# A batched 90-degree rotation: loads and stores on two queues with two pools of buffers, in place of one queue and units passed on

## The chip, the cores and the metric

The kernel runs on one core of one Trainium2 chip. The metric is the device time in microseconds (us). The kernel before was run six times; the median is 123.95 us.

## The reference

```python
def setup_inputs():
    batch, c, h, w = 32, 3, 256, 256
    return {"x": np.random.randn(batch, c, h, w).astype(np.float32)}

def reference(x):
    return np.rot90(x, k=-1, axes=(-2, -1)).astype(np.float32)
```

Each of the 96 images of 256 x 256 float32 values is turned by 90 degrees. Nothing is computed; 25.17 MB are read and 25.17 MB are written.

## The kernel before

The images are handled in 12 slabs of eight images, 2.10 MB each. A slab lies in SBUF as 128 partitions of 16 KB. It is loaded by two DMAs of 1 MB (`i` = 0 and 1), turned by two VectorE transposes of 128 x 2048 values, and stored to the output.

There are two forms of a slab. Slabs 0 and 11 (`last`) are loaded with 8 rows of an image in each partition (L63): a DMA is 128 pieces of 8 KB, and each of the two halves can be transposed by itself (L73). Slabs 1 to 10 are loaded with 16 rows in each partition (L65): a DMA is 64 pieces of 16 KB, one for every second partition, and a transpose (L79) needs both loads of its slab. Each of the two transposes of such a slab writes half of the columns `c` of both halves `i`, so both must be done before either half can be stored. Stores always go out in pieces of 8 KB, apart from the first.

All DMAs are issued by SyncE (SP), on one queue: first the 24 loads, then the stores in the order of the slabs 1 to 11, then slab 0. There is a buffer ("unit") for each of the 12 slabs, so no load waits for a buffer. Slab `n` is turned from its own unit into the unit of slab `n - 1`, whose data have been turned by then:

```python
t_in, t_out = units[n], units[n - 1] if n else turned0
```

Slab 0 has no unit before it: it is turned into `turned0` in PSUM. When slab 11 has been turned, ScalarE copies `turned0` into the unit of slab 11 (L92), from which slab 0 is stored at the very end (L93). Slab 1 is stored by three DMAs (L82 to L84), the first of which is short: 1 KB of each partition, 128 KB in all. Slabs 2 and 3 are stored by two DMAs each (L87), the others by one of 2 MB (L89).

The framework that builds the program sets the waits. It hands out eight semaphores for the completion of DMAs in turn. A DMA that gets a semaphore again waits, on its issuing engine, until the DMA that had it before has landed. With one queue that is the DMA eight places earlier.

Of the kernel before, what the change touches and what calls it, by code (L numbers as in the profile page):

```python
# [1 line left out]

# [4 lines left out]

@with_exitstack
def kernel(
    ctx: ExitStack,
    tc: tile.TileContext,
    x: bass.AP,
    out: bass.AP,
):

    nc = tc.nc
    fp32 = mybir.dt.float32

    B, C, H, W = x.shape
    P = nc.NUM_PARTITIONS  # L40
    RI, RO = 16, 8
    K = H // RI
    I = 2
    Q = P // (K * I)
    n_slabs = B * C // (Q * I)
    last = n_slabs - 1
    F = RO * W

    rows_in = x.rearrange("b c h w -> (b c h) w")
    rows_out = out.rearrange("b c h w -> (b c h) w")  # L50
    ld8_v = rows_in.rearrange("(n i p r) w -> n p i (r w)", i=I, p=P, r=RO)
    ld16_v = rows_in.rearrange("(n i m r) w -> n i m (r w)", i=I, m=Q * K, r=RI)
    st_v = rows_out.rearrange("(n i p c) w -> n p i (c w)", i=I, p=P, c=RO)

    pools = [ctx.enter_context(tc.tile_pool(name=f"unit{u}", bufs=1)) for u in range(n_slabs)]
    units = [pool.tile([P, I, F], fp32, name=f"u{u}") for u, pool in enumerate(pools)]
    psum = ctx.enter_context(tc.tile_pool(name="psum", bufs=1, space=bass.MemoryType.PSUM))
    turned0 = psum.tile([P, I, F], fp32, name="turned0")

    for n in range(n_slabs):  # L60
        for i in range(I):
            if n in (0, last):
                nc.sync.dma_start(out=units[n][:, i], in_=ld8_v[n][:, i])  # L63
            else:
                nc.sync.dma_start(out=units[n][i::I].rearrange("p i f -> p (i f)"), in_=ld16_v[n, i])  # L65

    for n in range(n_slabs):
        t_in, t_out = units[n], units[n - 1] if n else turned0
        if n in (0, last):
            for i in range(I):  # L70
                src = t_in[:, i].rearrange("p (r g c) -> p c r g", r=RO, c=RO)
                dst = t_out[:, i].rearrange("p (c g r) -> p c r g", c=RO, r=RO)
                nc.vector.transpose(out=dst[:, :, ::-1, ::-1], in_=src)  # L73
        else:
            src = t_in.rearrange("p i f -> p (i f)").rearrange("p (r g c) -> p c r g", r=RI, c=RO)
            dst = t_out.rearrange("p i (c k r) -> p c r k i", c=RO, r=RI)[:, :, ::-1, ::-1, :]
            for h in range(2):
                cs = slice(h * RO // 2, (h + 1) * RO // 2)
                nc.vector.transpose(out=dst[:, cs], in_=src[:, cs])  # L79

        if n == 1:
            nc.sync.dma_start(out=st_v[n][:, 0, :W], in_=t_out[:, 0, :W])  # L82
            nc.sync.dma_start(out=st_v[n][:, 0, W:], in_=t_out[:, 0, W:])
            nc.sync.dma_start(out=st_v[n][:, 1], in_=t_out[:, 1])  # L84
        elif n in (2, 3):
            for i in range(I):
                nc.sync.dma_start(out=st_v[n][:, i], in_=t_out[:, i])  # L87
        elif n:
            nc.sync.dma_start(out=st_v[n], in_=t_out)  # L89

    for i in range(I):
        nc.scalar.copy(out=units[last][:, i], in_=turned0[:, i])  # L92
    nc.sync.dma_start(out=st_v[0], in_=units[last])  # L93


# [1 line left out]
_INS = ['x']  # L97
_OUTS = [((32, 3, 256, 256), 'float32')]


# [23 lines left out]
```

## Time and profile before

| what | value |
|---|---|
| six runs | median 123.95 us, 123.61 to 124.03 |
| the profiled execution's own time | 123.88 us |
| its span in the profile | 122.1 us |
| VectorE (DVE) busy | 93.4 us (76%), 24 instructions |
| ScalarE (ACT) busy | 5.0 us (4%), 3 instructions |
| DMA | 50.33 MB, mean 412 GB/s over the span |

The span is the profiled part of that execution; 1.78 us of its own time lie around it. "DMA" in the profile is the mean busy share of the 16 DMA engines of the core, which carry out the transfers of every queue. "Packets" are the pieces that these engines move. An issue on SP ("SPq") only starts a transfer; "landing" is the time at which its completion was signalled.

### The profile page before, as it was taken

The page shows a single profiled execution, that of the slowest core. Times are in us where ns is not written, and L with a number is a line of the kernel's source. Part 1 is how long each engine was busy: PE and PEld are TensorE (multiplying, and loading weights), DVE is VectorE, ACT ScalarE, POOL GpSimd, SP SyncE. Part 2 cuts the span into 40 slices and gives each one's busy share as a digit, 9 for nine tenths or more (in the row PEclk, how much of TensorE's full clock was granted, in tenths as well). Part 3 has the DMA queues.
Part 4 walks back from the last instruction along what each step waited for, and adds up shares of the span by engine and source line. Part 5 has one row for each costly group of instructions (what it writes and reads, how often), then busy time and mean ns, then how long its engine had stood idle before and what let it go on. Part 6 is the DMA issues. An engine that isn't in the chain of part 4 may idle for free.

```text
span 122.1 us, 138 instructions
## 1 busy us (share of the span) xinstructions
DVE 93.4 (76%) x24; ACT 5.0 (4%) x3; POOL 0.2 (0%) x4
## 2 busy tenths in 40 slices
DVE  0199999999999999999999999999999950000000
ACT  0000000000000000000400000000000641000000
POOL 0000000000000000000000000000000000000000
DMA  3999999999999999999999999999999999999994
GB/s 89 429 432 429 429 429 429 429 429 429 429 429 429 429 429 429 429 429 421 384 402 430 427 427 429 429 429 429 427 427 429 429 427 429 427 429 429 429 427 180
DMA packets 5633, 50.33 MB, mean 412 GB/s; under 512 B 641, under 2 KB 769, under 8 KB 897
## 3 DMA queue, kind: packets, MB, share of 16 engines
q1 hardware_dynamic: 5632, 50.33, 97.8%
q14 instruction: 1, 0.00, 0.0%
HBM read 25.17 MB, written 25.17 MB: 412 GB/s over the span
## 4 chain that ended last, share of the span: by engine, by line
DVE 47%; issue 27%; DMA 4%; DVEq 3%; ACT 2%
DVE u L79 37%; DVE turned L73 6%; DMA u<-in_x_dram 4%; DVE u L73 3%; DVEq L119 3%; ACT u L92 2%
## 5 line engine op out<-in xcount | busy, mean ns | idle before, releaser
L79 DVE STREAM_TRANSPOSE u<-u 128x2048 f32<-128x2048 f32 x20 | 78.1, 3954 | 0.3
L73 DVE STREAM_TRANSPOSE turned<-u 128x2048 f32<-128x2048 f32 x2 | 7.6, 3830 | 5.5 <-DMA u<-in_x_dram 5.5
L73 DVE STREAM_TRANSPOSE u<-u 128x2048 f32<-128x2048 f32 x2 | 7.7, 3947 | 0.0
L92 ACT COPY u<-turned 128x2048 f32<-128x2048 f32 x2 | 3.7, 1865 | 36.7 <-DVE u L73 36.7
L92 ACT ACT_TABLE_LOAD x1 | 1.3, 1283 | 59.5 <-DMA u<-in_x_dram 59.5
L108 POOL MEMSET const-bfloat16-1.0<- 128x1 bf16 x1 | 0.1, 101 | 0.0
L108 POOL MEMSET const-uint8-127<- 128x1 uint8 x1 | 0.1, 101 | 0.0
L108 POOL MEMSET const-float32-0.0<- 128x1 f32 x1 | 0.1, 98 | 0.2 <-issue 0.2
L108 POOL MEMSET const-float32-1.0<- 128x1 f32 x1 | 0.1, 98 | 0.0
## 6 DMA issues: line engine op xcount, KB each, us to landing
u<-in_x_dram SPq DMA_DIRECT2D x24, 1024.0 KB, 19.6
out_dram<-u SPq DMA_DIRECT2D x9, 2048.0 KB, 22.9
out_dram<-u SPq DMA_DIRECT2D x5, 1024.0 KB, 17.8
out_dram<-u SPq DMA_DIRECT2D x1, 896.0 KB, 17.8
out_dram<-u SPq DMA_DIRECT2D x1, 128.0 KB, 18.2
```

The lines of the kernel that those rows point to most:

```text
L73: nc.vector.transpose(out=dst[:, :, ::-1, ::-1], in_=src)
L79: nc.vector.transpose(out=dst[:, cs], in_=src[:, cs])
L92: nc.scalar.copy(out=units[last][:, i], in_=turned0[:, i])
L108: nc = _bacc.Bacc("TRN2", target_bir_lowering=False, num_devices=1)
L119: with _tile.TileContext(nc) as tc:
```

## The change

The twelve units and the PSUM tile are replaced by two pools of six buffers each, `t_in` and `t_out`, every buffer 16 KB in each partition. Each slab takes a new buffer from both. SyncE issues the 24 loads, and ScalarE issues 24 stores of 1 MB each, in the order of the slabs from 0 to 11, each slab's two stores after its transposes. Slab 11 is loaded in the 16-row form; only slab 0 keeps the 8-row form. The three-part store of slab 1, the 2 MB stores, and the copies on ScalarE are gone.

```diff
-    pools = [ctx.enter_context(tc.tile_pool(name=f"unit{u}", bufs=1)) for u in range(n_slabs)]
-    units = [pool.tile([P, I, F], fp32, name=f"u{u}") for u, pool in enumerate(pools)]
-    psum = ctx.enter_context(tc.tile_pool(name="psum", bufs=1, space=bass.MemoryType.PSUM))
-    turned0 = psum.tile([P, I, F], fp32, name="turned0")
+    in_pool = ctx.enter_context(tc.tile_pool(name="in_pool", bufs=6))
+    out_pool = ctx.enter_context(tc.tile_pool(name="out_pool", bufs=6))
 
     for n in range(n_slabs):
-        for i in range(I):
-            if n in (0, last):
-                nc.sync.dma_start(out=units[n][:, i], in_=ld8_v[n][:, i])
-            else:
-                nc.sync.dma_start(out=units[n][i::I].rearrange("p i f -> p (i f)"), in_=ld16_v[n, i])
-
-    for n in range(n_slabs):
-        t_in, t_out = units[n], units[n - 1] if n else turned0
-        if n in (0, last):
+        t_in = in_pool.tile([P, I, RO * W], fp32, tag="t_in")
+        t_out = out_pool.tile([P, I, RO * W], fp32, tag="t_out")
+        if n == 0:
             for i in range(I):
+                nc.sync.dma_start(out=t_in[:, i], in_=ld8_v[n, i])
                 src = t_in[:, i].rearrange("p (r g c) -> p c r g", r=RO, c=RO)
                 dst = t_out[:, i].rearrange("p (c g r) -> p c r g", c=RO, r=RO)
                 nc.vector.transpose(out=dst[:, :, ::-1, ::-1], in_=src)
         else:
+            t_flat = t_in.rearrange("p i f -> p (i f)")
+            for i in range(I):
+                nc.sync.dma_start(out=t_flat[i::I], in_=ld16_v[n, i])
...
-        if n == 1:
-            nc.sync.dma_start(out=st_v[n][:, 0, :W], in_=t_out[:, 0, :W])
-            nc.sync.dma_start(out=st_v[n][:, 0, W:], in_=t_out[:, 0, W:])
-            nc.sync.dma_start(out=st_v[n][:, 1], in_=t_out[:, 1])
-        elif n in (2, 3):
-            for i in range(I):
-                nc.sync.dma_start(out=st_v[n][:, i], in_=t_out[:, i])
-        elif n:
-            nc.sync.dma_start(out=st_v[n], in_=t_out)
-
-    for i in range(I):
-        nc.scalar.copy(out=units[last][:, i], in_=turned0[:, i])
-    nc.sync.dma_start(out=st_v[0], in_=units[last])
+        for i in range(I):
+            nc.scalar.dma_start(out=st_v[n, i], in_=t_out[:, i])
```

In the built program the loads settle on four of the eight completion semaphores and the stores on the other four: a load waits for the load four places earlier, a store for the store four places earlier. There is one crossing: the eighth load (the second of slab 3) waits for the second store of slab 0.

More of the change, by code (lines that the diff above doesn't have):

```diff
@@ L45 @@
     n_slabs = B * C // (Q * I)
-    last = n_slabs - 1
-    F = RO * W
     rows_in = x.rearrange("b c h w -> (b c h) w")
     rows_out = out.rearrange("b c h w -> (b c h) w")
-    ld8_v = rows_in.rearrange("(n i p r) w -> n p i (r w)", i=I, p=P, r=RO)
+    ld8_v = rows_in.rearrange("(n i p r) w -> n i p (r w)", i=I, p=P, r=RO)
     ld16_v = rows_in.rearrange("(n i m r) w -> n i m (r w)", i=I, m=Q * K, r=RI)
-    st_v = rows_out.rearrange("(n i p c) w -> n p i (c w)", i=I, p=P, c=RO)
-    pools = [ctx.enter_context(tc.tile_pool(name=f"unit{u}", bufs=1)) for u in range(n_slabs)]
-    units = [pool.tile([P, I, F], fp32, name=f"u{u}") for u, pool in enumerate(pools)]
-    psum = ctx.enter_context(tc.tile_pool(name="psum", bufs=1, space=bass.MemoryType.PSUM))
-    turned0 = psum.tile([P, I, F], fp32, name="turned0")
-    for n in range(n_slabs):
-        for i in range(I):
-            if n in (0, last):
-                nc.sync.dma_start(out=units[n][:, i], in_=ld8_v[n][:, i])
-            else:
-                nc.sync.dma_start(out=units[n][i::I].rearrange("p i f -> p (i f)"), in_=ld16_v[n, i])
-    for n in range(n_slabs):
-        t_in, t_out = units[n], units[n - 1] if n else turned0
-        if n in (0, last):
+    st_v = rows_out.rearrange("(n i p c) w -> n i p (c w)", i=I, p=P, c=RO)
+    in_pool = ctx.enter_context(tc.tile_pool(name="in_pool", bufs=6))
+    out_pool = ctx.enter_context(tc.tile_pool(name="out_pool", bufs=6))
+    for n in range(n_slabs):
+        t_in = in_pool.tile([P, I, RO * W], fp32, tag="t_in")
+        t_out = out_pool.tile([P, I, RO * W], fp32, tag="t_out")
+        if n == 0:
             for i in range(I):
+                nc.sync.dma_start(out=t_in[:, i], in_=ld8_v[n, i])
                 src = t_in[:, i].rearrange("p (r g c) -> p c r g", r=RO, c=RO)
@@ L74 @@
         else:
-            src = t_in.rearrange("p i f -> p (i f)").rearrange("p (r g c) -> p c r g", r=RI, c=RO)
+            t_flat = t_in.rearrange("p i f -> p (i f)")
+            for i in range(I):
+                nc.sync.dma_start(out=t_flat[i::I], in_=ld16_v[n, i])
+            src = t_flat.rearrange("p (r g c) -> p c r g", r=RI, c=RO)
             dst = t_out.rearrange("p i (c k r) -> p c r k i", c=RO, r=RI)[:, :, ::-1, ::-1, :]
```

## The prediction

> **What bounds the kernel now.** I read the page first (slices, DMA queue, groups), then the stretches around the start, the middle and the end of the transfers, then SP's waits.
>
> ```profile
> DMA  3999999999999999999999999999999999999994
> GB/s 89 429 432 429 429 429 429 429 429 429 429 429 429 429 429 429 429 429 421 384 402 430 427 427 429 429 429 429 427 427 429 429 427 429 427 429 429 429 427 180
> DMA packets 5633, 50.33 MB, mean 412 GB/s; under 512 B 641, under 2 KB 769, under 8 KB 897
> ...
> q1 hardware_dynamic: 5632, 50.33, 97.8%
> ```
>
> The 16 DMA engines are full from the second slice to the last but one. One queue carries everything, so loads and stores never lie in the engines side by side, save at the crossing around 60 us.
>
> ```profile
> 20.00:30.00 10.00, 9.93 (x4) 0.00 (x0) 0.00 (x0) 1.00 1.00 426
> 75.00:85.00 10.00, 9.93 (x4) 0.00 (x0) 0.00 (x0) 1.00 1.01 429
> ```
>
> These are the stretches of loads alone and of stores alone (last columns: DMA share, GB/s). Both directions run at the same rate; I use 428 GB/s. 50.33 MB at that rate are 117.6 us.
>
> ```profile
> 58.00:59.00 1.00, 1.00 (x1) 0.00 (x0) 0.00 (x0) 1.00 0.99 410
> 59.00:60.00 1.00, 1.00 (x1) 0.52 (x1) 0.00 (x0) 1.00 0.98 369
> 60.00:61.00 1.00, 0.97 (x2) 0.77 (x1) 0.00 (x0) 1.00 0.99 369
> 61.00:62.00 1.00, 1.00 (x1) 0.00 (x0) 0.00 (x0) 1.00 0.96 365
> ...
> 120.50:120.75 0.25, 0.00 (x0) 0.00 (x0) 0.00 (x0) 1.00 0.24 98
> 120.75:121.00 0.25, 0.00 (x0) 0.00 (x0) 0.00 (x0) 1.00 0.01 0
> ```
>
> At the crossing the rate falls to about 368 GB/s for 3 us. By the page's slices 18 to 20 this costs (8 + 45 + 27) / 429 x 3.05 us = 0.57 us; by the three stretches 0.42 us. I use 0.5 us. The last data move at 120.6 us; the span ends 1.5 us later. So data begin at 120.6 - 117.6 - 0.5 = 2.5 us. Time = end of data + 1.5 + 1.78 (123.88 - 122.1). The profiled execution lies 0.07 us below the median of 123.95.
>
> ```profile
> 0.72 0.86 SPq L63 DMA_DIRECT2D u<-in_x_dram  x2
> ...
> 5.54 7.57 DVE L73 STREAM_TRANSPOSE turned<-u 128x2048 f32<-128x2048 f32 x2 [5.54 <-DMA u<-in_x_dram]
> ...
> L79 DVE STREAM_TRANSPOSE u<-u 128x2048 f32<-128x2048 f32 x20 | 78.1, 3954 | 0.3
> ...
> L92 ACT COPY u<-turned 128x2048 f32<-128x2048 f32 x2 | 3.7, 1865 | 36.7 <-DVE u L73 36.7
> ```
>
> From the first issue to the first data are 2.5 - 0.72 = 1.8 us. The first 1 MB (1.05 MB / 428 = 2.45 us) ends at 4.95, and DVE starts at 5.54: 0.6 us from last byte to the transpose. VectorE needs 7.93 us for a slab (two of 3.954 us and a gap), while the engines need 4.9 us for its loads and 4.9 us for its stores, 9.8 us together. DVE is not the bound, but it is 10.3 us (0.6 + 7.93 + 1.8) from a slab's last loaded byte to its first stored byte.
>
> ```profile
> SPq L65 <- DMA u<-in_x_dram: 25.5, 13, 2.0
> ```
>
> SP waits for the completion semaphore of the DMA eight places back, at up to 2.0 us a time. With eight DMAs of 1 MB in flight these waits cost nothing.
>
> **The change, part by part.**
>
> Gone, at nothing: the two copies of 1.87 us and the table load of 1.28 us on ScalarE. The last store was issued at 101.2 us and landed 20.1 us later, queued behind others all that time. Slab 11's other form changes nothing either (3947 against 3954 ns), nor do slab 0's transposes into SBUF (3830 to about 3947 ns, 0.2 us on an engine with 25 us to spare). If DVE became the bound, these 0.2 us would count.
>
> Gone, a gain: the crossing with its 128 pieces of 1 KB. The bounds are 0 and 0.57 us; I take 0.5, since no single place remains at which all engines turn.
>
> Issuing: 24 issues of about 0.35 to 0.47 us each on SP and on ACT, against 4.9 us of transfer for each pair. They are hidden; ACT has nothing else to do. A load now waits for the load four places back, so 4 MB are queued, 9.8 us of work even at the full rate, against 0.6 + 1.8 us to refill: nothing. The one crossing is the eighth load, which waits for slab 0's second store, and behind it on SP all later loads. With loads at two thirds of the rate (285 GB/s) and stores at one third (143): the stores start moving at 5.54 + 3.83 + 1.8 = 11.2 us, when 8.7 us x 428 GB/s = 3.7 MB are loaded. The seven loads before it (7.3 MB) end at 11.2 + 3.6 / 0.285 = 23.9 us; the two stores land at 11.2 + 2.1 / 0.143 + 0.6 = 26.5 us. The load ring is empty for about 4.4 us (2.6 + 1.8). Slab 1's stores, issued at 21 us, are 4.9 us of work at the full rate: covered, with little to spare.
>
> Buffers: at those rates the loads end at 11.2 + 21.45 / 0.285 = 86.5 us, when DVE has turned (86.5 - 5.5) / 7.93 = 10.2 slabs: under two slabs ahead, and six input buffers are enough. The out buffer of slab 10 is wanted at 84.8 us and free when slab 4 is stored, 11.2 + 10.5 / 0.143 + 0.6 = 85.2 us. That stall of 0.4 us is hidden by some 10 MB of waiting stores.
>
> What decides is how the engines divide themselves between the two rings. While anything is queued they do 428 GB/s, so only idle time at the end and a lower rate can cost. No idle time arises if, when the last byte is loaded, the stores queued or due from earlier slabs last through those 10.3 us: 4.4 MB, and slab 11's own 2.1 MB come after. So the loads must end by 2.5 + (50.33 - 6.5) / 0.428 = 104.9 us, which needs 21.45 MB / (104.9 - 11.2) = 229 GB/s, a share of 54% for loads. The packet row tells of pieces: 512 of 8 KB and 1280 of 16 KB for loads, 3200 for stores, with 40 x 16 = 640 completion writes, make 5632, the row's own number. So a load piece is 16 KB and a store piece 8 KB. If the engines take pieces in turn, loads get two thirds and the end is covered; if they share by bytes, loads get half and it is not.
>
> The Trainium skill, "DMA: Bandwidth & Descriptors", section "Queues, rings and completion order", says that an engine takes turns between rings by whole packets, and puts a packet at typically 9 to 17 descriptors. By that size a 1 MB store (8 pieces on an engine and a completion) would go in one turn, rings would share by bytes, and the sum would be the equal-share time below; with one piece to a packet it would be one of the other two. No run here shows which.
>
> The rate while both directions are mixed is not in this trace. From below it costs 0 (a gain is excluded: an engine's share is 0.99 to 1.03 busy in either direction alone). From above: the one place where directions meet ran at 368 instead of 428 GB/s, 16% more time; over the 75 us in which both rings are filled (11.2 to 86.5) that is 12 us. I take 2.7%, 2 us, far nearer to nothing, because the crossing also holds the 1 KB pieces and lasts only 3 us, and neither repeats. The same page, section "Latency and other measured facts", gives 214 GB/s in each direction for copies between HBM tensors; by that the mix would cost nothing and the time would be 123.4 us.
>
> Sum of the forecast: data end at 2.5 + 117.6 + 2.0 = 122.1; with 1.5 and 1.78 it is 125.4 us. The mix (0.4 to 4 us) gives 123.8 to 127.4.
>
> **The rivals.**
>
> *Loads ahead, mixing free: faster.* 2.5 + 117.6 + 1.5 + 1.78 = 123.4 us, the 0.5 us of the crossing gained. For it: both directions run at the same rate, and packets of 16 KB against 8 KB. Against: it has no room; a mix cost of 0.7% of 75 us takes all of it away. A measurement of this kernel can tell about 0.2% (0.25 us) from no change.
>
> *Equal shares: a hole at the end, slower.* Loads get half, a slab takes 9.8 us, and DVE (7.93) catches up within three slabs and then follows the loads. A slab's stores then begin 10.3 us after its last loaded byte, when the next slab has been loaded. At the end two slabs of stores (4.2 MB) are left: loads end at 2.5 + (50.33 - 4.2) / 0.428 = 110.3, slab 11's stores run from 120.6 to 125.5, and the time is 128.8 us. It decides below 54%; at 52% loads end at 11.2 + 21.45 / 0.223 = 107.4 and it is 107.4 + 10.3 + 4.9 + 3.3 = 125.9 us. In its favour: two rings of equal standing; against it: the sizes of the pieces.
>
> *It doesn't run side by side:* the eighth load's wait or a full pool stops the loads for long. If the 4.4 us above were not covered at all, the forecast becomes 129.8 us. The sizes of what is queued speak against it.
>
> **How the numbers follow.** Loads ahead with a mix cost: 0.40, of which 0.07 lies within 0.2% of before and 0.33 above. Loads ahead and mixing free: 0.28. Equal shares: 0.28. Loads stopped: 0.04. Faster is 0.28, same 0.07, slower 0.33 + 0.28 + 0.04 = 0.65. The forecast's own range is 123.8 to 127.4. The whole range goes from 123.2, a little below the free mix, to 128.9, the equal shares without a mix cost beside them; equal shares with one, the stopped loads and a gain beyond the crossing, some 0.15, are left out.
>
> **What would show it.** In the page after: two queues of 25 MB; the slices' rate from 11 to 87 us against 428 GB/s (420 or less for the forecast, 427 or more for the free mix); no dip at 60 us. The last load's landing tells the shares: near 87 us for two thirds, near 110 us for a half, and then DVE waits for loads from slab 3 on and one or two slices near the end are empty. DVE should end near 101 us in the first case and near 119 in the second. The forecast is wrong if the mixed stretch is as fast as before and no slice before the end is empty, or if DVE waits for loads throughout.

## The result and the profile after

The changed kernel takes 124.32 us (median of 22 runs, 123.79 to 124.79), the kernel before 123.9 us (46 runs). The ratio is 1.0032, 95% interval 1.0024 to 1.0040: slower by 0.3%, 0.42 us between the medians. The forecast had the direction (125.4 us, slower) but three and a half times the size. The profiled execution took 124.36 us, its span is 122.6 us.

The page after, slices and queues:

```profile
DMA  3999999999999999999999999999999999999993
GB/s 91 428 449 428 340 428 409 430 428 463 372 441 404 444 441 422 428 417 449 417 436 417 428 457 414 428 417 433 441 428 412 428 428 428 428 428 428 428 428 166
...
q1 hardware_dynamic: 2048, 25.17, 49.2%
q10 hardware_dynamic: 3456, 25.17, 48.6%
```

Two queues, 25.17 MB each, and engines that are full from the second slice to the last but one. The dip at 60 us is gone; two others stand in slice 4 (340) and slice 10 (372). Single slices scatter by 20 to 35 GB/s, since a piece is counted whole, where it starts; longer stretches are safer. These are the changed kernel's (the last two columns are the DMA share and GB/s):

```profile
10.00:20.00 10.00, 9.86 (x3) 0.00 (x0) 1.00 1.00 397
20.00:45.00 25.00, 19.79 (x6) 0.00 (x0) 1.00 1.01 426
45.00:70.00 25.00, 25.00 (x8) 0.00 (x0) 1.00 1.01 430
70.00:95.00 25.00, 25.00 (x7) 0.00 (x0) 1.00 1.00 427
```

And the same stretches of the kernel before:

```profile
10.00:20.00 10.00, 9.97 (x3) 0.00 (x0) 0.00 (x0) 1.00 0.99 423
20.00:45.00 25.00, 24.86 (x8) 0.00 (x0) 0.00 (x0) 1.00 1.01 430
45.00:70.00 25.00, 24.90 (x7) 1.28 (x1) 0.00 (x0) 1.00 1.00 418
70.00:95.00 25.00, 24.90 (x7) 0.00 (x0) 0.00 (x0) 1.00 1.01 427
```

From 45 us on the changed kernel moves loads and stores side by side at 427 to 430 GB/s, as fast as either alone. It loses (423 - 397) / 428 x 10 = 0.6 us from 10 to 20 us and 0.2 us from 20 to 45 us, and gains 0.7 us from 45 to 70 us, where the kernel before has its crossing. The rest of the difference (0.3 us) is in the first 10 us (331 against 338 GB/s) and in the last few; one profile doesn't carry differences of 0.1 us. In the bad stretches the DMA share stays at 1.00: the engines don't idle, their pieces take longer ("stretched" below). By the trace's records a load piece of 16 KB takes 611 ns elsewhere and up to 1035 ns from 11 to 15 us. Summed over all pieces and divided by 16 engines, the time over the usual duration is 0.70 us from 10 to 15 us, 0.24 us from 30 to 35 us, and 0.01 us or less in every other 5 us after the first five.

What the loads and VectorE waited for:

```profile
SPq L61 <- DMA out_dram<-t_out: 15.0, 1, 15.0
...
DVE t_out L66 <- DMA t_in<-in_x_dram: 5.2, 1, 5.2
```

The first line is the eighth load, waiting 15 us for slab 0's second store with all later loads behind it. In the trace's records no load piece starts between 23.5 and 29.8 us ("the loads' gap" below), and then no store piece between 30.2 and 32.9 us: slab 1's stores, alone in the engines, had ended, and slab 2's, issued at 29.0 us, moved their first piece only at 32.9 us. Slice 10 lies in this place. VectorE's wait (the second line) comes of the same gap, for slab 3's loads, and ends at 34.2 us; it did not make the stores run out, since slab 2 was turned by 29.0 us.

### The profile page after: what moved, and what is told of

Its sections match the earlier page's. It is cut to its first block, busy times and chain, and to the rows that moved or that the text cites. A ratio compares the mean times of both kernels' runs of the same rounds, so it can differ in the third digit from the quotient of the medians.

```text
span 122.6 us, 150 instructions
## 1 busy us (share of the span) xinstructions
DVE 92.3 (75%) x24; POOL 0.2 (0%) x4
## 3 DMA queue, kind: packets, MB, share of 16 engines
q1 hardware_dynamic: 2048, 25.17, 49.2%
q10 hardware_dynamic: 3456, 25.17, 48.6%
HBM read 25.17 MB, written 25.17 MB: 411 GB/s over the span
## 4 chain that ended last, share of the span: by engine, by line
DMA 63%; DVE 16%; DVEq 4%; SPq 1%; issue 0%
DMA t_in<-in_x_dram 53%; DMA out_dram<-t_out 10%; DVE t_out L66 9%; DVE t_out L57 6%; DVEq L95 3%; SPq L61 1%; DVEq L66 0%
## 5 line engine op out<-in xcount | busy, mean ns | idle before, releaser
L66 DVE STREAM_TRANSPOSE t_out<-t_in 128x2048 f32<-128x2048 f32 x22 | 84.6, 3946 | 5.3 <-DMA t_in<-in_x_dram 5.2
L57 DVE STREAM_TRANSPOSE t_out<-t_in 128x2048 f32<-128x2048 f32 x2 | 7.7, 3936 | 5.6 <-DMA t_in<-in_x_dram 5.6
```

## Experiments

The theory at first ("turns"): mixing is free, and each joining of a second direction costs some tenths of a microsecond. Rivals: a cost spread over the mixed stretch, the missing short first store, and the place (early in the kernel, or the first store of all). Ratios are against the kernel before, run beside it on the same chip, with 95% intervals.

**e1_nocross: the changed kernel without the loads' gap.** The loads are written four slabs ahead of the stores, and one edge is added to the order in which the framework hands out semaphores; it puts no wait into the program. Loads then only wait for loads.

```diff
+    AHEAD = 4
...
+    for n in range(AHEAD):
+        load(n)
...
+            if n == 0 and i == 1:
+                tc.add_manual_dep(store.ins, issued[1, 1].ins.name, mybir.DependencyInfo(mybir.DependencyClass.NoSync, mybir.DependencyReason.DATA), reason="order")
```

> The changed kernel with one edit: the fourth load (second of slab 1) is put ahead of slab 0's second store in the framework's order, so that the eighth load no longer waits for a store. Theory 'turns': the 0.42 us are lost where a direction joins the other in the engines, about 0.7 us where the stores join the loads (12 to 15 us) and about 0.3 us where the loads come back (30 to 34 us), against about 0.5 us at the one crossing of the kernel before; without the gap in the loads the second loss goes: 124.0 us, no stretch below 415 GB/s between 25 and 40 us, DVE's wait of 5.2 us gone. Rival 'spread': mixing costs 0.4 us evenly over the 80 us of both directions: 124.3 us, unchanged. Rival 'short store': the loss is the missing short first store: 124.3 us, unchanged.

123.84 us, 1.0004 (0.9987 to 1.0021). VectorE's wait of 5.2 us is gone, and so is the dip at 32 us; "spread" and "short store" had it unchanged. Run again beside the changed kernel (below), it gives the size.

**e11_changed and e12_nocross: the two side by side.**

> The changed kernel itself, on the same chip as the next one. Theory 'turns' and rival 'once' alike: 0.3 us over the next one, 0.4 us over the kernel before.

> The first experiment's kernel again, beside the changed kernel: 0.3 us under it, and within 0.15 us of the kernel before. If the gap in the loads had nothing to do with the loss, it equals the changed kernel.

The changed kernel 1.0037 (1.0025 to 1.0049), without the gap 1.0008 (0.9999 to 1.0016). So the gap costs 0.3%, 0.3 to 0.4 us, and what is left of the change is within 0.2% of the kernel before. The one row of e12_nocross in which SP's loads wait for a DMA, and its stretches:

```profile
SPq L60 <- DMA t_in<-in_x_dram: 61.5, 19, 4.4
...
10.00:20.00 10.00, 10.00 (x3) 0.00 (x0) 1.00 0.98 395
20.00:45.00 25.00, 25.00 (x8) 0.00 (x0) 1.00 1.02 432
```

From 20 to 45 us 432 instead of 426 GB/s: (432 - 426) / 432 x 25 = 0.35 us, the measured difference; e1_nocross has 432 too, and e11_changed 426. No piece is stretched near 32 us. The loss from 10 to 20 us is still there.

**e2_early: a store of 128 KB of zeros at the start of the changed kernel.**

```diff
+    nc.vector.memset(warm, 0.0)
+    nc.scalar.dma_start(out=st_v[0, 0][:, :W], in_=warm)
```

> The changed kernel with a store of 128 KB of zeros (1 KB of each partition) issued on ScalarE at the start, into rows that slab 0's first store overwrites later. Theory 'turns': the stores still join running loads at 12 us: the stretch there stays, 124.3 us or a little more. Rival 'cold start': the loss at 12 us is that of the first store of all (first use of ScalarE's queue, or first writes to the output); taken at the start it is gone from 12 to 15 us: 123.6 us if the start hides it, 124.3 us if it only moves there. Rival 'spread': 124.3 us.

124.61 us, 1.0054 (1.0030 to 1.0079): no faster than the changed kernel, and not clearly slower, since the intervals overlap. From 10 to 20 us the rate rose from 397 to 410 GB/s, but the first 5 us fell from 224 to 198 GB/s. Part of the loss moved to the start with the first store (stretched pieces cost 0.35 us from 10 to 20 us instead of 0.70); nothing was won.

**e3_pieces8: all loads in pieces of 8 KB.**

```diff
-        if n == 0:
+        if n >= 0:
```

> The changed kernel with all loads in the 8-row form, 128 pieces of 8 KB instead of 64 of 16 KB. If the engines take turns by pieces, loads and stores now share equally: DVE follows the loads and waits in every slab, the last load lands near 108 to 110 us, the DMA engines stand idle before the last slab's stores, 127.3 to 128.8 us. In this form a slab's halves are turned and stored one by one, so the hole can be shorter by half a slab, 3.9 us: 124.5 to 125. If they share by bytes or by whole transfers, the last load lands where it did in the changed kernel, about 94 us, and the time stays at 124.3 us.

124.35 us, 1.0042 (1.0027 to 1.0057). The time alone would fit the expectation's last case as well, in which the shares don't change; the last load, which ended at 110.7 us and not near 94, tells them apart. The page's queues, and then VectorE's waits:

```profile
q1 hardware_dynamic: 3456, 25.17, 49.4%
q10 hardware_dynamic: 3456, 25.17, 48.6%
```

```profile
DVE t_out L57 <- DMA t_in<-in_x_dram: 21.5, 18, 5.5
```

By the trace's records the engines moved 1827 load pieces and 1826 store pieces between 30 and 100 us: equal shares, 213.8 and 213.7 GB/s, and VectorE waits for a load 18 times. In the changed kernel, with 16 KB against 8 KB, there were 762 load and 842 store pieces from 40 to 85 us: 277 GB/s for loads and 153 for stores, a share of 64%. Equal counts don't show yet how long a turn is, but the order of the records does. On an engine a piece is booked 2 to 5 ns before the end of the piece ahead of it; from 40 to 85 us, 1691 ends have just one piece that starts there, and each time it belongs to the other queue. So the engines take the two queues in turn, one piece at a time. A completion write counts as a piece: on each engine 64 KB take 5 turns as loads and 9 as stores, which makes 9 / 14 = 64%. There was no hole at the end, as the expectation's half-slab chain allowed. What this kernel loses over e1_nocross fits its 1408 added pieces: two of 309 ns in place of one of 611 ns are 7 ns more, 1408 x 7 / 16 engines = 0.6 us.

**e7_equal_hole: equal shares, and transposes that need both loads.**

```diff
+            for h in range(2):
+                nc.vector.transpose(out=dst[:, :, cs], in_=src[:, :, cs])
```

> The third experiment's 8 KB pieces (loads and stores in equal shares) with the transposes of a slab split by columns, so that each needs both loads, as in the 16-row form. This is the prediction's rival of equal shares with its own chain: 10.3 us from a slab's last loaded byte to its first stored byte. By its sum the engines stand idle for 4 to 5 us before slab 11's stores: 128.3 to 129.4 us (128.8 and up to 0.6 for the smaller pieces). If the third experiment's lack of a hole has another cause than its shorter chain (6.4 us), there is none here: 124.4 us.

127.19 us, 1.0283 (1.0267 to 1.0298). The stretches near the end:

```profile
115.00:116.00 1.00, 1.00 (x1) 0.00 (x0) 1.00 0.97 410
116.00:117.00 1.00, 1.00 (x1) 0.00 (x0) 1.00 0.11 41
117.00:118.00 1.00, 1.00 (x1) 0.00 (x0) 1.00 0.00 0
118.00:119.00 1.00, 0.18 (x1) 0.00 (x0) 1.00 0.00 0
119.00:120.00 1.00, 0.00 (x0) 0.00 (x0) 1.00 0.96 393
```

The hole of the equal-shares rival exists; it is 3 us wide here, not the 4 to 5 us of the expectation, and costs 2.8 us over e3_pieces8. (Two of its loads also wait for stores, 15.5 us in all, but its last load ended at 109.7 us, no later than in e3_pieces8.) The changed kernel, with 16 KB load pieces, has no such hole.

**e4_noshort: the kernel before without its short first store.**

```diff
-            nc.sync.dma_start(out=st_v[n][:, 0, :W], in_=t_out[:, 0, :W])
-            nc.sync.dma_start(out=st_v[n][:, 0, W:], in_=t_out[:, 0, W:])
+            nc.sync.dma_start(out=st_v[n][:, 0], in_=t_out[:, 0])
```

> The kernel before without its short first store: slab 1 is stored by two DMAs of 1 MB. Rival 'short store': the crossing near 60 us costs 0.3 to 0.4 us more, 124.3 us. Theory 'turns': the crossing costs what it did, 123.9 us within 0.1. Rival 'spread': 123.9 us.

123.86 us, 1.0002 (0.9984 to 1.0019): the short first store is worth nothing that can be measured there.

**e10_short: the short first store in the kernel without the gap.**

```diff
+            if n == 0 and i == 0:
+                nc.scalar.dma_start(out=st_v[n, i][:, :W], in_=t_out[:, i, :W])
+                nc.scalar.dma_start(out=st_v[n, i][:, W:], in_=t_out[:, i, W:])
```

> The first experiment's kernel with the short first store of the kernel before: slab 0's first half goes out as 1 KB and then 7 KB of each partition. Rival 'short store' for the join at 12 us: the 0.7 us lost there shrink to 0.3 to 0.4, 123.5 us. Theory 'turns': the join costs the same whatever the first store's size: 123.8 to 123.9 us.

124.4 us, 1.0060 (1.0048 to 1.0072). The total doesn't tell what the run was made for: the added DMA shifts the semaphores, and a load waits for a store again (the first row below).

```profile
SPq L60 <- DMA out_dram<-t_out: 10.8, 1, 10.8
...
10.00:15.00 5.00, 5.00 (x2) 0.00 (x0) 1.00 1.01 427
15.00:20.00 5.00, 5.00 (x2) 0.00 (x0) 1.00 0.91 324
20.00:25.00 5.00, 5.00 (x3) 0.00 (x0) 1.00 1.02 432
25.00:30.00 5.00, 3.62 (x1) 0.00 (x0) 1.00 1.01 428
```

Its records tell two things. The short store's 1 KB pieces start at 13.5 us and no piece is stretched there; load pieces are stretched from 15.5 us (to 1114 ns, 0.71 us in all), ahead of the first 7 KB store pieces at 18.3 us. So the loss stands ahead of the first large store pieces, and the short store doesn't save it. And its loads stop from 17.9 to 22.9 us, just before the large store pieces come, which leaves the engines idle for some 0.25 us. When the loads are back, the stores run out from 23.2 to 24.7 us, as in the changed kernel, but no piece is stretched there, and the rate is full.

**e6_tiny: the kernel without the gap, and 16 pieces of 512 bytes at the start.** The edit is that of e2_early with `warm` of 16 x 128 values.

> The first experiment's kernel with a store of 16 pieces of 512 bytes of zeros issued on ScalarE at the start, into rows that slab 0's first store overwrites. Theory 'cold first store': of the 0.7 us lost at 12 us some 0.4 belong to the first store of all; in the second experiment they moved to the start (pieces stretched by 0.5 us per engine at 2 us) and 0.3 were left at 14 us. With 16 small pieces the cost at the start is smaller: 123.5 us, and the stretch at 12 us falls to 0.3 us. Rival 'moves': the cold part costs the same at any size: 123.8 to 124.0 us. Rival 'join only': the stretch at 12 us stays 0.7: 123.9 us.

123.81 us, 1.0014 (1.0004 to 1.0024). From 10 to 20 us 401 instead of 395 GB/s: stretched pieces cost 0.52 us from 10 to 15 us, against 0.53 in e12_nocross. A small early store takes nothing off the loss, so it is no matter of a first touch alone.

**e5_in2: two input buffers.**

```diff
-    in_pool = ctx.enter_context(tc.tile_pool(name="in_pool", bufs=6))
+    in_pool = ctx.enter_context(tc.tile_pool(name="in_pool", bufs=2))
```

> The first experiment's kernel (no gap in the loads at 25 us) with two input buffers instead of six, so that the loads of slab n + 2 wait for the transposes of slab n and the load ring runs empty for about 1.5 us in nearly every slab, about nine times. The engines stay full: the stores have 2 MB or more queued all the time, and 3.8 MB are left when slab 11's stores are due. Theory 'turns': every return of the loads costs 0.25 to 0.3 us: 123.8 + 9 x 0.27 = 126.3 us, with stretched load pieces after each gap. Rival 'once': the 0.3 us that went with the gap belong to its place in the start of the kernel, and a return in steady state is free: 123.8 to 124.0 us.

134.2 us, 1.0863 (1.0820 to 1.0907), 8 us more than "turns" gave. The expectation's ground was wrong: the engines were not kept full. In its trace (of an execution of 135.8 us) about 6 us of the added time are idle engines, most of it in a hole near the end, and about 6 us are stretched pieces of both directions in many places. The run can't price a single return of the loads. It shows that run-ahead of the loads is worth buffers.

**e8_units_act: the kernel before with its stores on ScalarE.** In the store block of the kernel before, `nc.sync.dma_start` becomes `nc.scalar.dma_start`.

> The kernel before with its stores issued on ScalarE instead of SyncE: two queues, but units, PSUM and the short first store as before. In its order of semaphores seven loads wait for a store (the ninth load for the first store, later ones for the stores of slabs 2 to 7), so the loads stop several times. Theory 'turns': 0.25 to 0.3 us for each return of the loads, five to seven of them: 125.0 to 125.9 us. Rival 'once': 123.9 to 124.1 us. A hole at the end would add to both and show as idle slices.

126.37 us, 1.0217 (1.0200 to 1.0234). SP waited 65.6 us in seven waits for stores. The trace's pieces are stretched around the end of the first of the loads' gaps (26 to 33 us), store pieces too, up to 664 ns, and the stores ran out there from 27.6 to 32.7 us; it costs some 1.5 us. After the three later long gaps, into full store queues, they are hardly stretched (0.03 us or less in 5 us). More time is lost near the end, with late loads: from 110 to 120 us the engines are 84% and 92% busy, at 351 and 382 GB/s. This spoke against "every return of the loads costs", and the next run tested it.

**e9_gap_late: the kernel without the gap, with one gap put into the steady stretch.**

```diff
+        if n == 6:
+            nc.gpsimd.memset(outs[2][0:1, 0, 0:1], 0.0)
+            nc.gpsimd.tensor_copy(out=t_in[0:1, 0, 0:1], in_=outs[2][0:1, 0, 0:1])
```

> The first experiment's kernel with one gap in the loads put into the steady stretch: the first load of slab 6 waits, by way of two one-element operations on GpSimd, until slab 2's first store has landed (one zero is written into its buffer after that; no output changes). The load ring runs empty for some 3 to 6 us near 45 us while the stores keep the engines full. Theory 'turns': the loads' return costs 0.25 to 0.3 us, 124.1 us, with stretched load pieces near 50 us. Rival 'once': the loss at 30 us belonged to the start of the kernel, a return in the steady stretch is free: the same as the kernel without the gap, 123.8 us.

123.85 us, 1.0020 (1.0010 to 1.0030), against 1.0008 (0.9999 to 1.0016) for e12_nocross, run beside it. No load piece starts between 42.4 and 49.9 us. The stretches around the loads' return:

```profile
45.00:50.00 5.00, 5.00 (x2) 0.26 (x2) 1.00 1.05 442
50.00:55.00 5.00, 1.84 (x1) 0.00 (x0) 1.00 1.03 439
55.00:60.00 5.00, 1.89 (x1) 0.00 (x0) 1.00 0.96 408
```

As many bytes as without the gap, and no stretched pieces. At most 0.1 to 0.2 us, less than half of what the early gap costs, though the gap is longer. "Turns" as first put fell here.

**e13_store_gap: a gap in the stores instead.** Here and in the next run the order of all DMAs is fixed by edges like that of e1_nocross, and loads wait for loads alone.

```diff
+                for _ in range(5 if n == 2 else 0):
+                    nc.scalar.copy(out=t_out, in_=t_out)
```

> The kernel without the loads' gap, with a gap in the stores instead: ScalarE copies slab 2's finished buffer onto itself five times (3.7 us each) before it issues slab 2's stores, so that the store ring runs empty from about 40 to 49 us while loads go on, and the stores then start again into running loads. The order of semaphores is that of the kernel without the loads' gap. Theory 'store start': the 0.3 us that the changed kernel loses at 32 us come from its stores, which ran dry behind the loads' gap (their pieces stop at 31.2 and start again at 33.8 us), joining running loads; here the same costs 0.25 to 0.7 us, 124.1 to 124.5 us, with load pieces stretched near 49 us. Rival 'loads' return': what costs is the loads coming back at 31 us; here they never stop: 123.8 us. Rival 'early': either is free in the steady stretch: 123.8 us.

123.82 us, 1.0008 (0.9999 to 1.0017). No store piece starts between 40.2 and 50.3 us; then the stores start into running loads:

```profile
45.00:50.00 5.00, 5.00 (x2) 1.81 (x1) 0.00 (x0) 1.00 1.00 429
50.00:55.00 5.00, 5.00 (x2) 0.00 (x0) 0.00 (x0) 1.00 1.03 439
```

No piece is stretched, and nothing is lost. The changed kernel's second loss is therefore not the stores' second start by itself. (The expectation gives the changed kernel's times by queue 1 us late; on the profile's clock they are 30.2 and 32.9 us.)

**e14_late_join: the first store held back.**

```diff
+            for _ in range(8 if (n, i) == (0, 0) else 0):
+                nc.scalar.copy(out=t_out[:, 0], in_=t_out[:, 0])
```

> The kernel without the loads' gap, with its first store held back: ScalarE copies the first half of slab 0 onto itself eight times (1.87 us each) before it issues the first store, so that the stores join the loads near 27 us instead of 14 us, once. Theory 'store start': the same 0.7 us are lost, at 25 to 28 us instead of 12 to 15 us: 123.8 us. Rival 'early': the loss at 12 us belongs to the start of the kernel and the join is free later: 123.1 to 123.4 us. Rival 'first store of all': as theory 'store start', it moves with the first store; the run before this one tells these two apart, by a second start of the stores.

123.79 us, 1.0006 (0.9997 to 1.0016). The stretch where the loss was, and the one to which it went:

```profile
10.00:20.00 10.00, 10.00 (x3) 9.84 (x6) 0.00 (x0) 1.00 1.02 434
25.00:30.00 5.00, 5.00 (x2) 0.10 (x1) 0.00 (x0) 1.00 0.99 365
```

The loss of (428 - 365) / 428 x 5 = 0.7 us moved to just ahead of the first store piece, at 29.6 us. With e13_store_gap, e6_tiny and e10_short it belongs to the first large store of the kernel, wherever that falls. The kernel before has the same sign, smaller: its 8 KB load pieces take up to 644 ns instead of 309 from 59.3 to 61.4 us, and its first store piece starts at 61.3 us. That store was issued at 44.8 us, so it is not its issue that slows the loads.

## Why the prediction was off

The direction, slower, came out right by luck: the term that made the forecast slower measured nothing, and a term that stood at nothing made the kernel slower. The prediction's own sign of being wrong came true, a mixed stretch as fast as before and no empty slice.

- **The mix, the term that failed.** The prediction took 2 us, from a range of 0 to 12 us whose upper end was the crossing's 368 GB/s stretched over the whole mixed time. It measured nothing: 427 to 430 GB/s from 45 to 95 us, and 428 with equal shares in e3_pieces8. The crossing was a single event and no sample of a mixed rate. The page's 428 GB/s for stores alone and loads alone was the better row. The Trainium skill, "DMA: Bandwidth & Descriptors", section "Latency and other measured facts", gives 214 GB/s per direction as the full rate of a copy between HBM tensors; e3_pieces8 shows 213.8 and 213.7.
- **The crossing, "gone, a gain" of 0.5 us.** It left 60 us, but the loss is that of the first large store and went with it: 0.6 us at 10 to 20 us in the changed kernel, 0.7 us at 25 to 30 us in e14_late_join. The net of this term is about nothing, as the ratio of e12_nocross, 1.0008, says.
- **The eighth load's wait, put at nothing.** The prediction saw the wait and its gap (24 to 28 us; it was 23.5 to 29.8 us) and priced only whether engines would idle. They did not, so that cover held, but the rate fell when the loads came back and the stores ran out; this is the 0.35 us that remain, nearly all of the measured 0.42 us. By its own terms the corrected sum is 125.4 - 2.0 + 0.5 + 0.35 = 124.25 us, against 124.32.
- **From issue to first piece, too short.** The prediction took 1.8 us everywhere, from the start of the kernel. Into engines that were busy with the other queue it was 3.4 to 4.5 us: the changed kernel's first store went from 9.6 to 13.8 us, its loads' return from 26.0 to 29.8 us, slab 2's stores from 29.0 to 32.9 us. Into idle engines it was 1.0 us for the first load and 0.8 us after the hole of e7_equal_hole. So the gap was two microseconds longer than forecast, and the stores, "covered, with little to spare", ran out at its end.
- **The shares: right.** The forecast had loads at two thirds by pieces; the trace has 64%, since the completion writes take turns too, and e3_pieces8 shows that the size of the piece decides. Without the gap the last load ended at 88.6 us (forecast 86.5); with it, 94.4 us. The Trainium skill, "DMA: Bandwidth & Descriptors", section "Queues, rings and completion order", puts a turn at typically 9 to 17 descriptors; on these two queues a turn was one piece (1691 times of 1691), so the measurement decides here.
- **The rival of equal shares** has a real mechanism, about 1.5 us over-priced (127.19 us where it had 128.8), and its condition was not met.
- **The free-mix rival** (123.4 us) had the right rate and missed both losses.
- **Buffers:** the stall of VectorE for slab 10's out buffer, 0.4 us in the prediction, shows in e1_nocross as 1.7 us in two waits and costs nothing, as said.

What stays open is the mechanism of the two losses. Pieces are stretched for two to four microseconds around the kernel's first large store, and, in the changed kernel, where loads stop until the stores run out as well. A return of loads alone (e9_gap_late) and a second start of stores alone (e13_store_gap), each in the steady stretch, cost less than half of the early gap or nothing; the same sequence of both in the steady stretch wasn't tried. In e10_short the sequence came early and no piece was stretched, so the sequence alone isn't enough; what else the changed kernel's gap has is not shown. That the gap costs the 0.3% is shown by e11_changed and e12_nocross. No version ran faster than the kernel before.

## What to carry to other kernels

Two directions on two queues cost no bandwidth here, so look at what the queues wait for instead: when a framework hands completion semaphores to both in turn, an added or shifted DMA can make a load wait for a store, and the order of the program with its waits shows this before any run. The size of the pieces set each queue's share in these runs, so give the direction that must run ahead the larger pieces. A dip at one event is not a rate: before it is spread over a stretch, ask what happens there only once.

## What the runs showed that was not expected

The first large store of this kernel slows the load pieces in flight for two to three microseconds before its own first piece appears: in the changed kernel they are stretched from 11.2 us on, and that piece starts at 13.8 us. This costs 0.6 to 0.7 us at 12 or 27 us and, by the prediction's three stretches, 0.4 us at 60 us, while the engines show as fully busy. The busy share alone would not have shown it; the GB/s of a stretch beside it did.
